# Second block's attention: two heads handled together, their score and value products issued in turns

## The chip, the cores and the metric

The kernel runs on one core of a Trainium2 chip. A core has a matrix engine (TensorE, called PE in the profile, with its weight loads listed apart as PEld), a vector engine (DVE), an activation engine (ACT), a small general engine (POOL) and a queue engine (SP) that starts most transfers from the chip's memory (HBM). Each engine has its own instruction queue and works through it in order; semaphores tie the queues together. The metric is the time in microseconds (us) that one execution takes on the device, and the median of several executions is compared.

## The reference

A sequence of 256 tokens of width 1024 in float32 runs through two layers of a first block and then one layer of a second block. The change touches the second block only. Cut to what matters there:

```python
# second_block, one layer: x is (256, 1024)
h = rmsnorm(x, g_mix_pre) * (1 + scale_m) + shift_m      # scale, shift, gate: from a condition vector
q, k, v, u = split(h @ w_in, 4)                           # each (256, 512)
# attention, 8 heads of width 64, strictly causal, "stick breaking":
z = q @ k.T / 8;  log1m = where(s < t, -softplus(z), 0)
after = reverse_cumsum(log1m) - log1m
w = where(s < t, exp(log_sigmoid(z) + after), 0)
attn = w @ v
# pooling: 4 groups of 128 channels of u, windows 2, 4, 8, 16
pooled[g] = trailing_mean(u[g], window[g]) - u[g];  pool[g] = (pooled[g] @ w_pool[g]) * pool_scale[g]
x = x + gate_m * rmsnorm(concat(attn, pool) @ w_out, g_mix_post)
h = rmsnorm(x, g_ffn_pre) * (1 + scale_f) + shift_f
x = x + gate_f * rmsnorm((silu(h @ w_gate) * (h @ w_up)) @ w_down, g_ffn_post)
```

## The kernel before

**Weights.** All large weights lie in HBM in one packed array, in the order of use (`ORDER`), in chunks of two halves of 128 x 1024. SP loads each half into one of 7 `raw` buffers (L258). ACT then makes a rounded copy H (L278) and DVE the rest L = raw - H (L280), each in one of 12 buffers, so that a product with a float32 weight is made of H and L parts in a faster matmul type. Activations are split the same way (`Pair`, L185 to L213). `get(key, cap)` (L284) hands out the next chunk, and on the way emits the loads up to 5 chunks ahead and the splits up to 3 chunks ahead, or up to the half numbered `cap` where one is given. `behind` (L262) makes the splits queue up after a named instruction of ACT (index 0) and of DVE (index 1), which is kept in `state["behind"]`.

**Order of the work.** The program's text is one long list of instructions. Small jobs that are to be woven into a long row of matmuls are generators: `spawn(gen, delay)` puts one on a list with a due time on a clock that `pe(ns)` moves on by an estimate of TensorE's time, and `tick()`, called between batches of matmuls, runs those that are due up to their next `yield`, whose value is the next delay. `drain()` runs all that is left. A scheduler then puts the instructions into the engines' queues by priority, which is their place in the text, and may let a later instruction that is ready go ahead of one that is not. `tc.high_priority(offset=PRIO)`, in the helper `hp`, moves instructions 30 places up.

**The second block's mixer** (`mixer2`, L981). For each half of the tokens, t = 0 and 1, `mmA4` makes q and then k (24 matmuls of 512 columns each, in batches of four H and two L). `turn` (L991) copies the result to memory on ACT (L993), transposes it on TensorE (L997) and copies it into `qT` or `kT` on DVE (L999). Then come v and u, for two halves of the tokens each (`pv`, `pu`), and into these rows of matmuls the eight heads are woven.

**A head** (`stick`, L938; `hp` is a pair of heads, `e` the head in it): two score matmuls into a PSUM tile `z`, with 64 rows of contraction, which lie on partitions 0 to 63 for e = 0 and 64 to 127 for e = 1; a mask addition on DVE (L949); Abs, Exp, Ln on ACT (L951 to L953); a combination on DVE (L955); three matmuls with a triangle of -1 (`tri`) that form the running sums in the same PSUM tile; Exp on ACT (L962) to `wT`. Each head is a generator of its own, spawned 3.5 clock units after the one before. When both of a pair are through, the value products are issued: all of e = 0, then all of e = 1, into the partitions 0 to 63 and 64 to 127 of one PSUM tile `po`. ACT and DVE put them, split, into the mixer's output `mp` (L211, L212).

**Pooling** (`pool`, L1024): for each of four groups in a row, a matmul pair into `pl`, a copy on ACT (L1031), a matmul with `wpool` into `ppl`, and a scaled split on ACT and DVE (L1037, L1038).

**After the mixer**: `w_out`, chunks of the pooled channels first (L1131), `drain()`, then the chunks of the attention's channels; norms; then the feed-forward part (`ffn`, L528). `gated` (L1107) loads a row of gains and a row of the modulation through ACT's DMA queue and multiplies them on DVE (128 x 1024). The last such row, `Pf`, is made before the feed-forward part starts (L1146) and is used only at its end. `ffn` has a parameter `early`, a function called at the seventh of the eleven chunks of the down product (L577); the first block's layers make their rows there.

Of the kernel before, what the change touches and what calls it, by code (L numbers as in the profile page):

```python
# [12 lines left out]
AF = mybir.ActivationFunctionType  # L13
# [5 lines left out]
P = 128  # L19
D = 1024  # L20
T = 256
# [4 lines left out]
HD = 64  # L26
# [22 lines left out]
UNIT = 10.0  # L49
SM_DELAY = 8.0  # L50
SOFT = 30
ST_DELAY = 7.0
ST_STEP = 3.5


# [107 lines left out]
def tile_model(ctx: ExitStack, tc: tile.TileContext, x_in, wpack, sink, convw, gains, c_in,  # L163
               b_cond, w_pool, pool_scale, ident_c, rope_c, amask_c, smask_c, tri_c, pmat_c, out):
    nc = tc.nc
# [7 lines left out]
    def s4(name, shape=(P, D), dt=F32):  # L173
        return ac.tile(list(shape), dt, tag="s4", name=name, bufs=NS4)

    def s2(name, shape=(P, 512), dt=F32):
        return ac.tile(list(shape), dt, tag="s2", name=name, bufs=NS2)

    def ps1(name, shape=(P, 512), dt=F32):
        return pp.tile(list(shape), dt, tag="B", name=name, bufs=8)  # L180
# [38 lines left out]
    def spawn(gen, delay=0.0):  # L219
        tasks.append([clock[0] + delay, gen])  # L220

    def pe(ns):
        clock[0] += ns / 1000.0
# [22 lines left out]
    def mm(o, a, b, start, stop, **kw):  # L246
        nc.tensor.matmul(o, a, b, start=start, stop=stop, **kw)  # L247


    state = dict(raw=0, spl=0, use=0, behind=None, a=None, v=None)  # L250
# [33 lines left out]
    def get(key, cap=None):  # L284

        i = state["use"]
        assert ORDER[i] == key, (ORDER[i], key)
        n = len(ORDER)
        while state["raw"] < 2 * min(i + LOOK_RAW, n):
            emit_raw()  # L290
        ahead = min(i + LOOK, n) * 2
        if cap is not None:
            ahead = max(min(cap, 2 * n), 2 * i + 2)
        while state["spl"] < ahead:
            emit_half()
        state["use"] += 1
        return HL.pop(i)
# [57 lines left out]
    def hp():  # L355
        return nullcontext() if state["use"] <= 4 else tc.high_priority(offset=PRIO)


    def sumsq(src, c, ssq, name):

        junk = s2(f"jk_{name}{c}")
        nc.scalar.activation(junk, src, AF.Square, scale=D ** -0.5, accum_out=ssq[:, c:c + 1])
        return nc.scalar.activation(ssq[:, c:c + 1], ssq[:, c:c + 1], AF.Identity,
                                    bias=eps if c == 0 else ssq[:, 0:1])
# [570 lines left out]
        return mp  # L935


    def stick(hp, qT, kT, v2, mp, psz, pend):  # L938
        ws = [None, None]

        def head(e):
            r = slice(e * HD, (e + 1) * HD)
            z = psz(hp, e)
            mm(z[:, 0:T], kT[r, hp, 0:P], qT[r, hp, :], True, False, skip_group_check=True)
            mm(z[:, T:T + P], kT[r, hp, P:T], qT[r, hp, P:T], False, False, skip_group_check=True)
            pe(650)
            zz = z[:, 0:384]
            z3 = zz.rearrange("p (b t) -> p b t", b=3)
            nc.vector.tensor_add(z3[:, 0:3:2, :], z3[:, 0:3:2, :], smask.unsqueeze(1).to_broadcast([P, 2, P]))  # L949
            e1 = s2(f"e1_{hp}{e}", (P, 384))  # L950
            nc.scalar.activation(e1, zz, AF.Abs)  # L951
            nc.scalar.activation(e1, e1, AF.Exp, scale=-1.0)
            nc.scalar.activation(e1, e1, AF.Ln, bias=1.0)  # L953
            spf = s2(f"sp{hp}{e}", (P, 384))
            nc.vector.scalar_tensor_tensor(spf, zz, 0.0, e1, ALU.max, ALU.add)  # L955
            yield ST_DELAY
            mm(z[:, 0:T], tri[:, 0, :], spf[:, 0:T], False, False, skip_group_check=True)
            mm(z[:, P:T], tri[:, 1, :], spf[:, T:T + P], False, False, skip_group_check=True)
            mm(z[:, T:T + P], tri[:, 0, :], spf[:, T:T + P], False, True, skip_group_check=True)
            pe(870)  # L960
            wT = s2(f"wT{hp}{e}", (P, 384))
            nc.scalar.activation(wT, zz, AF.Exp)  # L962
            ws[e] = wT
            yield 2.0
            if ws[0] is None or ws[1] is None or pend[hp]:
                yield None
                return
            pend[hp] = True
            po = ps1(f"po2{hp}")
            for ee in range(2):  # L970
                o = po[ee * HD:(ee + 1) * HD, :]
                vs = slice((2 * hp + ee) * HD, (2 * hp + ee + 1) * HD)
                mm(o[:, 0:T], v2[0][:, vs], ws[ee][:, 0:T], True, False, skip_group_check=True)
                mm(o[:, P:T], v2[1][:, vs], ws[ee][:, T:T + P], False, True, skip_group_check=True)
            pe(730)
            mp.put(hp, 1, po[:, 0:T].unsqueeze(1))
            yield None

        return [head(0), head(1)]

    def mixer2(xp, norms):  # L981
        mp = Pair("m2")
        qT = s4("qT2", (P, 4, T))
        kT = s4("kT2", (P, 4, T))
        v2t = s4("v2", (P, 2, 512))
        u2t = s4("u2", (P, 2, 512))
        v2 = [v2t[:, t, :] for t in range(2)]
        cap = 2 * state["use"] + 8
        ww = {n: [get((n, h), cap) for h in range(2)] for n in ("q2", "k2")}

        def turn(nm, t, ps, dstT, scl):  # L991
            tk = s2(f"tk2{nm}{t}")
            nc.scalar.activation(tk, ps, AF.Copy, scale=scl)  # L993
            yield 1.5
            pt = ps1(f"pt2{nm}{t}", (P, 4, P))
            for k in range(4):
                nc.tensor.transpose(pt[:, k, :], tk[:, k * P:(k + 1) * P], ident)  # L997
                pe(107)
            nc.vector.tensor_copy(dstT[:, :, t * P:(t + 1) * P], pt)  # L999
            yield None  # L1000

        for t in range(2):
            finish(norms[t].gen)
            for nm, dstT, scl in (("q2", qT, 0.125), ("k2", kT, 1.0)):
                ps = ps1(f"p2{nm}{t}")
                mmA4(ps, ww[nm], xp, t)
                spawn(turn(nm, t, ps, dstT, scl))
                tick()
        pend = [False] * 4

        def psz(hp, e):
            return ps1(f"z{hp}{e}")

        for hp in range(4):
            for e, gen in enumerate(stick(hp, qT, kT, v2, mp, psz, pend)):
                spawn(gen, 3.0 + ST_STEP * (2 * hp + e))
        for n, dst in (("v2", v2t), ("u2", u2t)):
            w = [get((n, h)) for h in range(2)]
            for t in range(2):
                ps = ps1(f"p{n}{t}")  # L1020
                mmA4(ps, w, xp, t)
                nc.scalar.copy(dst[:, t, :], ps)

        def pool(g):  # L1024
            pl = ps1(f"pl{g}")
            gs = slice(g * P, (g + 1) * P)
            mm(pl[:, 0:T], u2t[:, 0, gs], pmat[g // 2][:, g % 2, 0:T], True, False, skip_group_check=True)
            mm(pl[:, P:T], u2t[:, 1, gs], pmat[g // 2][:, g % 2, T:T + P], False, True, skip_group_check=True)
            pe(650)
            pm = s2(f"pm{g}", (P, T))  # L1030
            nc.scalar.copy(pm, pl[:, 0:T])  # L1031
            yield 1.5
            ps = ps1(f"ppl{g}")
            mm(ps[:, 0:T], wpool[:, g, :], pm, True, True)
            pe(432)
            h = mp.k(0, 4 + g)
            nc.scalar.activation(h, ps[:, 0:T], AF.Copy, scale=pscale[:, g:g + 1])  # L1037
            nc.vector.scalar_tensor_tensor(mp.k(1, 4 + g), ps[:, 0:T], pscale[:, g:g + 1],  # L1038
                                           h.bitcast(F32), ALU.mult, ALU.subtract)
            yield None  # L1040

        for g in range(4):
            for _ in pool(g):
                pass
        return mp


# [1 line left out]
    xp = Pair("x0")  # L1049
    norms = None  # L1050

    for l in range(DEPTH):
        mp = mixer1(l, xp, norms)
        gpm, gpf = row(4 * l + 1, f"gpm{l}"), row(4 * l + 2, f"gpf{l}")
        xp = Pair(f"xf{l}")
        norms = [Norm(t, gpf, None, xp, f"nf{l}{t}") for t in range(2)]
# [50 lines left out]
    def gated(gi, mi, name, one):  # L1107
        g = row(gi, "g" + name)
        m = s4("m" + name)
        nc.scalar.dma_start(m, modd[mi].partition_broadcast(P))  # L1110
        if one:
            nc.vector.scalar_tensor_tensor(g, m, 1.0, g, ALU.add, ALU.mult)
        else:
            nc.vector.tensor_mul(g, g, m)  # L1114
        return g

    mp = mixer2(xp, norms)
    xp = Pair("xf2")
# [4 lines left out]
    norms = [Norm(t, Gf, Sf, xp, f"nf2{t}") for t in range(2)]  # L1123
# [12 lines left out]
    cap = 2 * (state["use"] - 2) + NSPLIT  # L1136
    aw = [(get(("wo", 2, j), cap), mp.ks(0, 2 * j, 2), mp.ks(1, 2 * j, 2)) for j in (0, 1)]
    for t in range(2):
# [4 lines left out]
                mmD2(accs[t], *ch, t, c, len(left) == 2 and i == 0, ch is aw[1])  # L1143
            post.half(c)
        after3(t, post)
    Pf = gated(11, 5, "pf2", False)  # L1146

    def fin(t, post):
        def put(c):
            nc.sync.dma_start(out[t * P:(t + 1) * P, HC[c]], xt[t][:, HC[c]])  # L1150
        post.fin(put)

    ffn(2, xp, norms, lambda t, acc: Post(t, acc, Pf, f"pf2{t}"), fin)


def _consts():
# [56 lines left out]
```

## Time and profile before

| what | value |
|---|---|
| median of 3 executions | 1161.8 us (1160.68 to 1162.2) |
| the profiled execution, its own time | 1160.45 us |
| its span, first to last instruction | 1158.3 us |
| mean granted TensorE clock | 0.999 |
| PE busy / PEld busy | 1143.9 / 956.8 us |
| DVE busy / ACT busy | 801.3 / 687.5 us |
| transfers on SP's queue | 224.83 MB |

Times in the profile are counted from the span's start. A line of the timeline gives the start, the time until the last of the merged instructions ends, the engine, the source line, the operation, the tiles written and read (out<-in), the shape, how many were merged, and in brackets how long the engine sat idle before and what ended that. A matmul's shape begins with rows * columns of the array that it uses: `128*128` is the whole array, `64*128` half of its rows, `128*64` half of its columns. Nearly all matmuls stand under L247, a helper, so they are told apart by their tiles. A float32 matmul that is not split into H and L shows as two records.

### The profile page before, as it was taken

How to read it: one execution, taken by the hardware profiler on the slowest of the kernel's cores; microseconds unless marked ns; L12 is line 12 of the kernel's file. 1: busy time of each engine (PE TensorE's matmuls, PEld its weight loads, DVE VectorE, ACT ScalarE, POOL GpSimd, SP SyncE). 2: the span in 40 equal slices, each digit the busy share in tenths (PEclk: the TensorE clock that was granted, in tenths of full speed). 3: DMA queues.
4: the chain of work that ended last, by engine and by line, in shares of the span. 5: the costliest groups of instructions: out<-in, count | busy, mean ns of one | idle time of the engine just before them, and what ended most of it. 6: DMA issues, size and time to landing. Idle time of an engine off the chain costs nothing. (4 is left out here: it accounts for less than half of the span.)

```text
span 1158.3 us, 16004 instructions
## 1 busy us (share of the span) xinstructions
PE 1143.9 (99%) x5917; PEld 956.8 (83%) x5917; DVE 801.3 (69%) x1190; ACT 687.5 (59%) x1211; POOL 13.5 (1%) x28
## 2 busy tenths in 40 slices
PE   9999999999999999999999999999999999999997
PEld 5898888888888888888888888888887777888886
DVE  7888845858877647889855659966678437865642
ACT  6777865547545546688856456544556646645441
POOL 0000000000000000000000000000000000000000
PEclk9999999999999999999999999999999999999999
DMA  8934346737987854744575629977856343855600
GB/s 290 354 130 149 124 150 208 264 123 282 339 269 240 260 172 134 266 145 147 184 251 181 218 75 316 331 245 253 273 188 217 128 147 125 313 193 181 203 22 37
DMA packets 67039, 235.39 MB, mean 203 GB/s; under 512 B 8849, under 2 KB 9361, under 8 KB 66962
## 3 DMA queue, kind: packets, MB, share of 16 engines
q1 hardware_dynamic: 63216, 224.83, 56.9%
q10 hardware_dynamic: 3746, 9.56, 2.4%
q8 instruction: 46, 0.75, 0.3%
q14 instruction: 31, 0.25, 0.1%
HBM read 233.28 MB, written 1.07 MB: 202 GB/s over the span
## 5 line engine op out<-in xcount | busy, mean ns | idle before, releaser
L280 DVE TENSOR_TENSOR L<-raw,H 128x1024 fp32r<-128x1024 f32 x370 | 444.8, 1220 | 139.6 <-ACT H L278 132.0
L278 ACT CAST H<-raw 128x1024 fp32r<-128x1024 f32 x370 | 382.9, 1051 | 141.3 <-DMA raw<-in_wpack_dram 33.3
L247 PE MATMUL dn<-H,fHL 128*128 128x512 f32 x432 | 116.1, 390 | 0.0
L247 PE MATMUL pu<-xf,H 128*128 128x512 f32 x432 | 108.2, 392 | 0.0
L247 PE MATMUL pg<-xf,H 128*128 128x512 f32 x432 | 107.8, 391 | 0.0
L247 PEld LDWEIGHTS dn<-H,fHL 128*128 128x128 f32 x432 | 79.8, 188 | 15.6
L247 PEld LDWEIGHTS pg<-xf,H 128*128 128x128 f32 x432 | 79.2, 188 | 15.2
L247 PEld LDWEIGHTS pu<-xf,H 128*128 128x128 f32 x432 | 77.7, 189 | 13.9
L522 DVE SCALAR_TENSOR_TENSOR raw<-raw,silu_c 128x1024 f32<-128x1024 f32 x48 | 58.2, 1219 | 35.2 <-DMA raw<-in_wpack_dram 35.2
L247 PE MATMUL dn<-L,fHL 128*128 128x512 f32 x216 | 66.6, 389 | 0.0
L247 PEld LDWEIGHTS pg<-xf,L 128*128 128x128 f32 x432 | 58.9, 190 | 4.2
L247 PEld LDWEIGHTS pu<-xf,L 128*128 128x128 f32 x432 | 58.9, 190 | 4.2
L247 PE MATMUL pu<-xf,L 128*128 128x256 f32 x432 | 60.2, 282 | 0.0
L247 PE MATMUL pg<-xf,L 128*128 128x256 f32 x432 | 60.2, 282 | 0.0
L569 ACT CAST fHL<-f 128x512 fp32r<-128x512 f32 x27 | 16.7, 620 | 60.2 <-DVE f L567 60.2
L247 PE MATMUL wo<-H,m 128*128 128x512 f32 x192 | 52.3, 394 | 0.0
L563 ACT ACTIVATE s<-s 128x512 f32<-128x512 f32 x27 | 17.1, 631 | 54.6 <-DVE s L456 54.6
L247 PEld LDWEIGHTS dn<-L,fHL 128*128 128x128 f32 x216 | 40.5, 188 | 8.6
L247 PEld LDWEIGHTS wo<-H,m 128*128 128x128 f32 x192 | 35.5, 188 | 7.2 <-issue 0.2
L247 PE MATMUL pcp<-H,y 128*128 128x512 f32 x128 | 35.2, 395 | 0.0
L247 PE MATMUL pap<-H,o 128*128 128x512 f32 x128 | 35.1, 394 | 0.0
L664 ACT ACTIVATE P<-S,nm 128x256 f32<-128x256 f32 x64 | 29.6, 480 | 8.9 <-DVE nm L658 6.4
(290 smaller groups left out, 1950.3 us busy)
## 6 DMA issues: line engine op xcount, KB each, us to landing
raw<-in_wpack_dram SPq DMA_DIRECT2D x422, 512.0 KB, 5.4
gpm<-in_gains_dram ACTq DMA_DIRECT2D x3, 512.0 KB, 7.4
gpf<-in_gains_dram ACTq DMA_DIRECT2D x3, 512.0 KB, 8.9
gqf<-in_gains_dram ACTq DMA_DIRECT2D x2, 512.0 KB, 6.5
out_dram<-x SPq DMA_DIRECT2D x4, 256.0 KB, 2.0
pmat<-in_pmat_dram SPq DMA_DIRECT2D x2, 384.0 KB, 7.5
x<-in_x_dram SPq DMA_DIRECT2D x2, 256.0 KB, 2.9
x<-in_x_dram SPq DMA_DIRECT2D x1, 512.0 KB, 6.9
```

The lines of the kernel that those rows point to most:

```text
L247: nc.tensor.matmul(o, a, b, start=start, stop=stop, **kw)
L278: nc.scalar.copy(H, r)
L280: nc.vector.tensor_sub(L, r, H.bitcast(F32))
L522: nc.vector.scalar_tensor_tensor(w[u], w[u], 1.0, silu_c, ALU.mult, ALU.mult, accum_out=mcol[:, r, 2 * j + u:2 * j + u + 1])
L563: last = nc.scalar.activation(s, s, AF.Silu)
L569: nc.scalar.copy(fHL[:, 0], fv)
L664: nc.scalar.activation(Pt[:, hh, :], S[hh // 2][:, hh % 2, :], AF.Exp, bias=nm[:, hh:hh + 1], accum_out=den[:, hh:hh + 1])
```

## The change

The two heads of a pair become one generator. The score matmuls are issued e = 0, e = 1, e = 0, e = 1, and so are the value products. The three triangle matmuls of a head become two: one over 384 columns in place of one over 256 and one over 128. `spf` is written over `e1`. A pair is spawned every 7 units, as before on average, and the delay between scores and triangles is 8.0 in place of 7.0. In `turn`, the copies on ACT and DVE get the raised priority, and weight splits queue behind the copy on ACT. The split of v's weights is asked for in the first half of the tokens, right after k; u's weights are asked for after v's products and with a cap that ends at u's own halves, so `w_out`'s splits are emitted later than before. The first matmul pair of the next pooled group is issued before the second matmul of the current one. `Pf` is made through `early`.

```diff
-ST_DELAY = 7.0
+ST_DELAY = 8.0
...
+    ahead = hp
...
-    def stick(hp, qT, kT, v2, mp, psz, pend):
...
+    def stick(hp, qT, kT, v2, mp):
+
+        rs = [slice(e * HD, (e + 1) * HD) for e in range(2)]
+        z = [ps1(f"z{hp}{e}") for e in range(2)]
+        for e in range(2):
+            mm(z[e][:, 0:T], kT[rs[e], hp, 0:P], qT[rs[e], hp, :], True, False, skip_group_check=True)
+        for e in range(2):
+            mm(z[e][:, T:T + P], kT[rs[e], hp, P:T], qT[rs[e], hp, P:T], False, False, skip_group_check=True)
+        pe(900)
+        sps = []
+        for e in range(2):
...
-            spf = s2(f"sp{hp}{e}", (P, 384))
+            spf = e1
             nc.vector.scalar_tensor_tensor(spf, zz, 0.0, e1, ALU.max, ALU.add)
-            yield ST_DELAY
-            mm(z[:, 0:T], tri[:, 0, :], spf[:, 0:T], False, False, skip_group_check=True)
-            mm(z[:, P:T], tri[:, 1, :], spf[:, T:T + P], False, False, skip_group_check=True)
-            mm(z[:, T:T + P], tri[:, 0, :], spf[:, T:T + P], False, True, skip_group_check=True)
+            sps.append(spf)
+        yield ST_DELAY
+        ws = []
+        for e in range(2):
+            spf = sps[e]
+            mm(z[e][:, 0:384], tri[:, 0, :], spf, False, False, skip_group_check=True)
+            mm(z[e][:, P:T], tri[:, 1, :], spf[:, T:T + P], False, True, skip_group_check=True)
             pe(870)
             wT = s2(f"wT{hp}{e}", (P, 384))
-            nc.scalar.activation(wT, zz, AF.Exp)
-            ws[e] = wT
...
+            nc.scalar.activation(wT, z[e][:, 0:384], AF.Exp)
+            ws.append(wT)
+        yield 2.0
+        po = ps1(f"po2{hp}")
+        vs = [slice((2 * hp + e) * HD, (2 * hp + e + 1) * HD) for e in range(2)]
+        for e in range(2):
+            mm(po[rs[e], 0:T], v2[0][:, vs[e]], ws[e][:, 0:T], True, False, skip_group_check=True)
+        for e in range(2):
+            mm(po[rs[e], P:T], v2[1][:, vs[e]], ws[e][:, T:T + P], False, True, skip_group_check=True)
...
             tk = s2(f"tk2{nm}{t}")
-            nc.scalar.activation(tk, ps, AF.Copy, scale=scl)
+            with ahead():
+                state["behind"] = (nc.scalar.activation(tk, ps, AF.Copy, scale=scl), state["behind"][1])
...
-            nc.vector.tensor_copy(dstT[:, :, t * P:(t + 1) * P], pt)
+            with ahead():
+                nc.vector.tensor_copy(dstT[:, :, t * P:(t + 1) * P], pt)
...
+                if t == 0 and nm == "k2":
+                    wv = [get(("v2", h), cap + 4) for h in range(2)]
         for hp in range(4):
-            for e, gen in enumerate(stick(hp, qT, kT, v2, mp, psz, pend)):
-                spawn(gen, 3.0 + ST_STEP * (2 * hp + e))
+            spawn(stick(hp, qT, kT, v2, mp), 3.0 + 2 * ST_STEP * hp)
         for n, dst in (("v2", v2t), ("u2", u2t)):
-            w = [get((n, h)) for h in range(2)]
+            w = wv if n == "v2" else [get((n, h), cap + 8) for h in range(2)]
...
+        gens = [pool(g) for g in range(4)]
+        next(gens[0])
         for g in range(4):
-            for _ in pool(g):
-                pass
+            if g < 3:
+                next(gens[g + 1])
+            next(gens[g])
...
-    Pf = gated(11, 5, "pf2", False)
+    Pf = []
...
-    ffn(2, xp, norms, lambda t, acc: Post(t, acc, Pf, f"pf2{t}"), fin)
+    ffn(2, xp, norms, lambda t, acc: Post(t, acc, Pf[0], f"pf2{t}"), fin,
+        lambda: Pf.append(gated(11, 5, "pf2", False)))
```

More of the change, by code (lines that the diff above doesn't have):

```diff
@@ L935, in mixer1 @@
         return mp
-    def stick(hp, qT, kT, v2, mp, psz, pend):
[L939 to L947, printed above, removed]
+    def stick(hp, qT, kT, v2, mp):
[8 more added lines that the diff above has]
+        for e in range(2):
+            zz = z[e][:, 0:384]
             z3 = zz.rearrange("p (b t) -> p b t", b=3)
@@ L953, in head @@
             nc.scalar.activation(e1, e1, AF.Ln, bias=1.0)
-            spf = s2(f"sp{hp}{e}", (P, 384))
+            spf = e1
             nc.vector.scalar_tensor_tensor(spf, zz, 0.0, e1, ALU.max, ALU.add)
-            yield ST_DELAY
-            mm(z[:, 0:T], tri[:, 0, :], spf[:, 0:T], False, False, skip_group_check=True)
-            mm(z[:, P:T], tri[:, 1, :], spf[:, T:T + P], False, False, skip_group_check=True)
-            mm(z[:, T:T + P], tri[:, 0, :], spf[:, T:T + P], False, True, skip_group_check=True)
+            sps.append(spf)
[5 more added lines that the diff above has]
+            mm(z[e][:, P:T], tri[:, 1, :], spf[:, T:T + P], False, True, skip_group_check=True)
             pe(870)
             wT = s2(f"wT{hp}{e}", (P, 384))
-            nc.scalar.activation(wT, zz, AF.Exp)
-            ws[e] = wT
[L964 to L979, printed above, removed]
+            nc.scalar.activation(wT, z[e][:, 0:384], AF.Exp)
[7 more added lines that the diff above has]
+            mm(po[rs[e], P:T], v2[1][:, vs[e]], ws[e][:, T:T + P], False, True, skip_group_check=True)
+        pe(730)
+        mp.put(hp, 1, po[:, 0:T].unsqueeze(1))
+        yield None
     def mixer2(xp, norms):
@@ L1008, in mixer2 @@
                 tick()
-        pend = [False] * 4
-        def psz(hp, e):
-            return ps1(f"z{hp}{e}")
+                if t == 0 and nm == "k2":
+                    wv = [get(("v2", h), cap + 4) for h in range(2)]
         for hp in range(4):
-            for e, gen in enumerate(stick(hp, qT, kT, v2, mp, psz, pend)):
-                spawn(gen, 3.0 + ST_STEP * (2 * hp + e))
+            spawn(stick(hp, qT, kT, v2, mp), 3.0 + 2 * ST_STEP * hp)
         for n, dst in (("v2", v2t), ("u2", u2t)):
-            w = [get((n, h)) for h in range(2)]
+            w = wv if n == "v2" else [get((n, h), cap + 8) for h in range(2)]
             for t in range(2):
```

## The prediction

> **What bounds the kernel now.** The page comes first, for the busy times.
>
> ```profile
> span 1158.3 us, 16004 instructions
> PE 1143.9 (99%) x5917; PEld 956.8 (83%) x5917; DVE 801.3 (69%) x1190; ACT 687.5 (59%) x1211; POOL 13.5 (1%) x28
> ```
>
> TensorE is never idle for long, so a microsecond taken from its queue is a microsecond of the span, as long as no other engine's work becomes late for it. Whether that holds behind the mixer is read from the chain of waits in order of time: from the end back to 976 it is TensorE alone (and the last norm), and before that stands a piece of DVE:
>
> ```profile
> 973.62 1.23 DVE gpf L1114
> 974.84 1.15 DVE L L280
> 975.99 0.04 issue
> 976.03 3.44 PE puA L247 x14
> ```
>
> So time won in the mixer (866 to 942) is passed on to the end. What is left is to see how much of TensorE's time in the mixer is streaming and how much is entry, exit and waiting, and how full its helpers are. Busy time by stretches, the mixer from v's first product on and the feed-forward part:
>
> ```profile
> 890.30:942.00 51.70, 49.15 (x230) 36.67 (x229) 25.04 (x35) 30.63 (x55) 0.00 (x0) 1.00 0.46 163
> 990.60:1158.00 167.40, 160.84 (x845) 138.13 (x843) 92.18 (x114) 75.75 (x116) 1.10 (x2) 0.99 0.45 154
> ```
>
> (Columns: length; busy PE, PEld, DVE, ACT, POOL with counts; clock; DMA share; GB/s.) ACT is busy for 30.63 of 51.70 us there, DVE for 25.04: room, though not endless.
>
> **The change part by part.** TensorE's timeline gives each insertion's price: the time between the starts of the rows around it, less what these rows take undisturbed. First the undisturbed rows, with one insertion of value products behind them:
>
> ```profile
> 946.95 0.62 PE L247 MATMUL wo<-L,m 128*128 128x512 f32 x2
> 947.41 1.07 PE L247 MATMUL wo<-H,m 128*128 128x512 f32 x4
> 948.31 0.61 PE L247 MATMUL wo<-L,m 128*128 128x512 f32 x2
> 948.86 0.88 PE L247 MATMUL po<-wT,v 128*64 128x256 f32 x8
> 949.66 1.67 PE L247 MATMUL wo<-H,m 128*128 128x512 f32 x6
> 951.17 0.63 PE L247 MATMUL wo<-L,m 128*128 128x512 f32 x2
> ```
>
> Two L matmuls take 947.41 - 946.95 = 0.46 us and four H matmuls 0.90 undisturbed. The eight `po` records of the last pair were put into the queue in turns already, and both heads took 949.66 - 948.86 = 0.80 together; the way in cost 948.86 - 948.31 - 0.46 = 0.09, the way out 951.17 - 949.66 - 1.35 = 0.16 (six H matmuls would be 1.35): **1.05 us for a pair in turns**. The other pairs were not so:
>
> ```profile
> 911.75 1.04 PE L247 MATMUL z<-sp,tri 128*128 128x256 f32 x6
> 912.72 1.51 PE L247 MATMUL po<-wT,v 128*64 128x256 f32 x8
> 914.17 1.19 PE L247 MATMUL pu<-H,xm 128*128 128x512 f32 x4
> 915.20 0.63 PE L247 MATMUL pu<-L,xm 128*128 128x512 f32 x2
> ...
> 922.36 0.86 PE L247 MATMUL po<-wT,v 128*64 128x256 f32 x4
> 923.15 0.92 PE L247 MATMUL z<-qT,kT 64*128 64x256 f32 x4
> ...
> 924.42 0.86 PE L247 MATMUL po<-wT,v 128*64 128x256 f32 x4
> ...
> 932.14 0.86 PE L247 MATMUL po<-wT,v 128*64 128x256 f32 x4
> ...
> 934.00 0.86 PE L247 MATMUL po<-wT,v 128*64 128x256 f32 x4
> ```
>
> The first pair, one head after the other, took 914.17 - 912.72 = 1.45, with 0.09 in and 1.03 - 0.90 = 0.13 out: 1.67. Two pairs had their heads at different places, each 0.79 (923.15 - 922.36) + 0.09 + 0.13 = 1.01. **Value products**: before 1.67 + 4 x 1.01 + 1.05 = 6.8, after 4 x 1.05 = 4.2, a gain of 2.6.
>
> **Scores.** Each of the eight heads has an insertion of its own, on half of the rows of the array:
>
> ```profile
> 900.36 0.61 PE L247 MATMUL pv<-L,xm 128*128 128x512 f32 x2
> 900.90 0.92 PE L247 MATMUL z<-qT,kT 64*128 64x256 f32 x4
> 901.75 1.20 PE L247 MATMUL pv<-H,xm 128*128 128x512 f32 x4
> 902.79 0.62 PE L247 MATMUL pv<-L,xm 128*128 128x512 f32 x2
> ```
>
> That is 902.79 - 900.36 - 0.46 - 0.90 = 1.07 us, eight times 8.6. No row shows two heads on the two row halves in turns. Bounds from the nearest rows: if they overlap as the column halves do (0.80 for both against 0.79 for one), a pair costs 1.08, four cost 4.3, and the gain is 4.2. If the second head is streamed after the first, it adds what the second head of `po` added, 1.45 - 0.79 = 0.66; a pair costs 1.73, four cost 6.9, and the gain is 1.6, from half the entries alone. I take 4.2: the two halves are the same kind of split, and the heads write different PSUM tiles.
>
> In the Trainium skill, TensorE: Matmul & The Clock Gate, "The mechanism" of its part on packing, weight loads overlap running matmuls only where the row groups differ; the column halves above overlapped all the same, so the trace is the better judge here. The same page, "Measured speedup vs the span model", has four row tiles at 3.07 times, not 4. With the same share (1.53 of 2, an estimate from that page) a score pair would stream 2 x 0.85 / 1.53 = 1.11 in place of 0.85, and the gain would be 3.2 in place of 4.2.
>
> **Triangles.** Six records become four over the same 1024 columns (twice 256 + 128 + 128, twice 384 + 128). Six took 912.72 - 911.75 = 0.97 us, and `po`'s eight in sequence took 1.45 for 1536: in both 0.95 per 1000, so time goes with columns and the gain is 0. The other end: two records of six, 0.32 a head, 2.6 in all.
>
> **The wait for k's copy.** ACT's row, then TensorE's:
>
> ```profile
> 891.86 1.05 ACT L278 CAST H<-raw 128x1024 fp32r<-128x1024 f32 x1 [2.32 <-DMA raw<-in_wpack_dram]
> ...
> 894.10 0.59 ACT L993 ACTIVATE tk2k<-p2k 128x512 f32<-128x512 f32 x1
> ```
>
> ```profile
> 894.74 0.66 PE L997 MATMUL pt2k<-ident,tk2k 128*128 128x128 f32 x4 [1.61 <-ACT tk2k L993]
> ```
>
> The copy of k stood in ACT's queue behind splits that waited for a transfer, and the transposes stood at the head of TensorE's queue. With raised priority, and u's splits made to queue behind it, the copy comes first: gain 1.6, at worst 0. What is late next is u's splits: four pairs that wait until k's copy is through (about 890.3), needed when u starts, some 12 us later; ACT needs 4 x 1.05 for them. SP's queue keeps the order of its loads; while u's splits wait, its seven buffers stay full and the loads pause, which the DMA share of 0.46 in this stretch leaves room to make up. POOL's queue is not touched.
>
> **Pooled groups.** Two of the four second products waited:
>
> ```profile
> 939.59 0.70 PE L247 MATMUL ppl<-pm,wpool 128*128 128x256 f32 x2 [0.46 <-ACT pm L1031]
> ...
> 941.40 0.70 PE L247 MATMUL ppl<-pm,wpool 128*128 128x256 f32 x2 [0.46 <-ACT pm L1031]
> ```
>
> With the next group's first pair between, the wait is covered, except for the last group, which has only the group before it in front: 0.9 less about 0.2 is 0.7. Bounds 0 and 0.9.
>
> **The last gain row.** Its product is the 1.23 us of `gpf` in the chain above. It delays the split that TensorE waits for:
>
> ```profile
> 975.19 0.48 PE L247 MATMUL pgA<-H,xf 128*128 128x512 f32 x1
> 976.03 0.72 PE L247 MATMUL puA<-L,xf 128*128 128x512 f32 x2 [0.36 <-DVE L L280]
> ```
>
> A matmul that takes 0.23 (0.46 / 2) held the queue for 0.84: gain 0.6; the split would start 1.2 earlier, so nothing remains of this wait. Two DMA issues go from ACT's queue with it. At its new place DVE is busy for 92.18 of 167.40 us, and the splits are made three chunks ahead; that is the cover. Without it, the step can hold DVE as its model in the layer before did:
>
> ```profile
>   DMA scl_m<-modd: 8.1, 1
> ```
>
> 8.1 us of waiting for a row at L1078, ahead of which TensorE shows no wait. I take 0.
>
> **New waits.** The splits that move are the cost. ACT's casts (L278) by stretches:
>
> ```profile
> 878.00:890.30 12.30, 9.88 (x10) 1.00 0.63 194
> 890.30:942.00 51.70, 10.44 (x10) 1.00 0.46 163
> ```
>
> Of the ten before 890.3, v's four remain; u's four and w_out's first two come later. ACT then has 30.63 + 6 x 1.04 = 36.9 us in a stretch of 51.70 - 9.1 (the gains above without the last) = 42.6: 87%, DVE 25.04 + 6 x 1.22 = 32.4: 76%. A pair's chain runs through both. One head's, with two casts in between:
>
> ```profile
> 902.32 0.49 ACT L951 ACTIVATE e<-z 128x384 f32<-128x384 f32 x1 [0.69 <-DVE z L949]
> ...
> 905.32 0.52 ACT L953 ACTIVATE e<-e 128x384 f32<-128x384 f32 x1
> ```
>
> ```profile
> 906.59 0.55 DVE L955 SCALAR_TENSOR_TENSOR sp<-z,e 128x384 f32<-128x384 f32 x1
> ```
>
> From the end of the scores (901.75) to 907.14 are 5.4 us; the second head's three steps on ACT add 1.5, so 6.9, against a delay of 8.0 units. A slack of 1.1, about one cast. Bounds for the waits at the triangles: 0, and 4.0 (16 casts spread over four pairs are two more each, 2.1 - 1.1 = 1.0 a pair). I take 0.7, near the lower end, since w_out's splits come later in the text than the chains and yield to them.
>
> **Sum**: 4.2 + 2.6 + 1.6 + 0.7 + 0.6 - 0.7 = 9.0 us. The profiled execution took 1160.45, its span 1158.3: 1151.4 for such a one. It lies 1.35 below the median of the runs, so against the median: 1161.8 - 9.0 = **1152.8 us**.
>
> **The rivals.** *Row halves do not overlap.* For it: no row shows them together. Against it: the column halves do. The scores give 1.6 in place of 4.2: 1155.4.
>
> *ACT becomes the bound of the mixer.* For it: 87%, and one cast of slack per pair. Against it: u's splits have 12 us. The waits are 4.0 in place of 0.7: 1156.1.
>
> *The queue does not follow the text.* The last pair's value products went in turns though the text had them in sequence, so the scheduler's order counts, and it may cut a pair's insertion in two. Eight insertions cut would each cost a way in and out again, 0.09 + 0.13, and a first load of about 0.1: 8 x 0.3 = 2.6, so 1155.4.
>
> *Slower: the pair's chain is late at every pair.* Both heads' triangles now stand behind one chain that goes through ACT six times and through DVE ahead of and behind that. If on top of the four casts a pair also meets two of DVE's L (1.22 each), 1.0 + 2.4 = 3.4 us are exposed per pair, with TensorE's queue standing at the triangles: 4 x 3.4 = 13.8 against 9.7 gained: 1165.9. It decides from 9.7 / 4 = 2.4 us per pair on. Against it: v's and u's matmuls stand between scores and triangles by the due times, and splits of lower priority do not go first where a chain's step is ready.
>
> **How the numbers follow.** Forecast 0.55, row halves 0.18, ACT 0.14, cut insertions 0.05, slower 0.04; the last 0.04 for a gain of more than 11.5 (triangles cheaper by some of their 2.6). Range: below, no new waits and part of the triangles' gain, 1152.8 - 0.7 - 2.3 = 1149.8; above, past the rivals at 1155.4 and 1156.1, 1156.6. It leaves out the slower case and joint misses. About 0.2% (2.3 us) can be told from no change; faster 0.91 (all cases but the last and joint misses), same 0.05, slower 0.04.
>
> **What would show it.** Right: four score insertions `64*128` of eight records, with about 0.85 us from the start of one to the next row, and four `po` insertions of 0.80; no wait for `tk2k`; no DVE `gpf` ahead of `puA`; the mixer shorter by about 8 us, and the feed-forward part the same length. Row halves wrong: score insertions of 1.5. ACT: TensorE idle ahead of `z<-sp,tri` or `pu`, ended by L955, L953 or L280. Wrong altogether: a feed-forward part that starts earlier and then waits for splits.

## The result, and the profile after

The changed kernel takes 1149.42 us (median of 4 executions, 1148.9 to 1150.55) against 1161.24 us before (4 executions, 1160.56 to 1162.2). The ratio is 0.9906, with a 95% interval of 0.9895 to 0.9917, which is 9.6 to 12.2 us less; the two medians alone differ by 11.8. 1152.8 was forecast, 9.0 less than a median of 1161.8. The direction was right, and the gain was larger than the sum of its terms. As a time, 1149.42 lies 0.4 below the lower end of the stated range, 1149.8 to 1156.6. As a gain it lies inside: from 1161.8 that range is 5.2 to 12.0 us less. The profiled execution took 1148.9 us, its span 1146.9.

The head of the page of the changed kernel:

```profile
span 1146.9 us, 15965 instructions
...
PE 1135.7 (99%) x5901; PEld 951.2 (83%) x5901; DVE 799.9 (70%) x1190; ACT 686.9 (60%) x1211; POOL 13.4 (1%) x28
```

Sixteen matmul records fewer are the triangles. TensorE's own work fell by 8.2 us (1143.9 to 1135.7), and the span by 11.4, so some waiting went as well. Busy time by stretches (length; PE, PEld, DVE, ACT, POOL with counts; clock; DMA share; GB/s) of the changed kernel, from v's first product to the first of `w_out`, and the feed-forward part:

```profile
889.60:929.45 39.85, 39.78 (x205) 30.39 (x205) 27.67 (x37) 33.49 (x61) 0.00 (x0) 1.00 0.63 211
979.80:1147.00 167.20, 160.88 (x845) 138.17 (x843) 92.95 (x115) 75.45 (x116) 1.10 (x2) 0.99 0.47 159
```

The first stretch was 51.70 us long before and TensorE was busy for 49.15 of it; now it is 39.85 long and TensorE is idle for 0.07 of it. Not all of the difference is won: two pairs' value products now stand behind the first row of `w_out`, where one pair's stood before. The feed-forward part is as long as before. Where each stage begins is read from the first matmul record of its tile on TensorE's timeline, and the differences are what the experiments are compared by. All kernels in one table, in us, with the experiments that come below:

| kernel | v to u | u | u's end to w_out | w_out and norm | gate/up, first chunk | feed-forward | last matmul to end | q's first to end |
|---|---|---|---|---|---|---|---|---|
| before | 17.61 | 23.96 | 9.94 | 23.99 | 24.70 | 160.61 | 7.24 | 292.23 |
| changed | 13.51 | 19.78 | 6.54 | 25.85 | 24.37 | 160.61 | 6.62 | 281.55 |
| e1_sequence | 13.64 | 19.80 | 6.53 | 26.10 | 24.38 | 160.61 | 6.62 | 281.86 |
| e2_pairs_only | 15.21 | 19.78 | 8.81 | 25.02 | 24.89 | 160.61 | 7.23 | 285.73 |
| e3_rest_only | 15.39 | 24.34 | 7.75 | 25.49 | 24.33 | 160.62 | 6.62 | 288.72 |
| e4_pool_sequence | 13.52 | 19.78 | 8.81 | 25.02 | 24.30 | 160.62 | 6.62 | 282.86 |
| e5_same_due | 16.01 | 18.82 | 10.10 | 24.33 | 25.46 | 160.62 | 7.29 | 286.84 |
| e6_no_priority | 14.04 | 19.78 | 6.54 | 25.80 | 24.33 | 160.61 | 6.62 | 281.91 |
| e7_row_old_place | 13.52 | 19.78 | 6.53 | 25.83 | 25.31 | 160.61 | 7.25 | 283.02 |
| e8_apart | 15.53 | 21.20 | 8.92 | 27.05 | 24.36 | 160.62 | 6.63 | 288.49 |
| e9_row_only | 16.39 | 23.96 | 9.94 | 24.01 | 24.31 | 160.62 | 6.62 | 290.04 |
| e10_tighter_step | 15.17 | 19.35 | 6.49 | 23.96 | 24.35 | 160.62 | 6.61 | 280.74 |
| e11_changed_again | 13.51 | 19.78 | 6.54 | 25.83 | 24.31 | 160.62 | 6.61 | 281.48 |

The columns run from start to start: from the first `pv` to the first `pu`, on to the last `pu`, to the first `wo`, to the first `pgA`, to the first `pg`, to TensorE's last matmul, and from there to the end; the 24.2 to 24.3 us of q and k ahead of them are in the last column only. Each row is one execution; the changed kernel's two (changed and e11) differ by 0.07 in the last column. From q's first matmul on the change saves 292.23 - 281.55 = 10.68 us in these two executions; 0.7 more lies ahead of q, where nothing was changed, and moves by as much between executions of one kernel.

TensorE's timeline of the changed kernel, one pair's scores alone, and one pair's scores with the value products of another behind them:

```profile
900.25 0.61 PE L247 MATMUL pv<-L,xm 128*128 128x512 f32 x2
900.80 0.92 PE L247 MATMUL z<-qT,kT 64*128 64x256 f32 x8
901.65 1.20 PE L247 MATMUL pv<-H,xm 128*128 128x512 f32 x4
902.69 0.62 PE L247 MATMUL pv<-L,xm 128*128 128x512 f32 x2
...
904.53 1.90 PE L247 MATMUL z<-e,tri 128*128 128x384 f32 x8
...
908.58 0.61 PE L247 MATMUL pu<-L,xm 128*128 128x512 f32 x2
909.13 0.92 PE L247 MATMUL z<-qT,kT 64*128 64x256 f32 x8
909.98 0.87 PE L247 MATMUL po<-wT,v 128*64 128x256 f32 x8
910.78 1.19 PE L247 MATMUL pu<-H,xm 128*128 128x512 f32 x4
911.81 0.63 PE L247 MATMUL pu<-L,xm 128*128 128x512 f32 x2
...
934.37 0.62 PE L247 MATMUL wo<-L,m 128*128 128x512 f32 x2
934.92 0.65 PE L247 MATMUL po<-wT,v 128*64 128x256 f32 x2
935.50 1.20 PE L247 MATMUL wo<-H,m 128*128 128x512 f32 x4
936.53 0.62 PE L247 MATMUL wo<-L,m 128*128 128x512 f32 x2
...
939.58 0.86 PE L247 MATMUL po<-wT,v 128*64 128x256 f32 x6
```

Eight score records take 901.65 - 900.80 = 0.85 us, the time that four took before, and the whole insertion 902.69 - 900.25 - 0.46 - 0.90 = 1.08. The two row halves overlap to within 0.01 us. Where the value products stand right behind the scores (twice), the two share one way in and out: 911.81 - 908.58 - 0.46 - 0.90 = 1.87 for both, where 1.08 + 1.05 = 2.13 was forecast. Against that, one pair's value products are cut in two, two records at 934.92 and six at 939.58.

The chain of waits of the changed kernel where it reaches the feed-forward part, in order of time:

```profile
960.54 1.41 DVE xg_nf L395 x2
961.96 1.15 DVE L L280
963.10 0.04 issue
963.15 3.52 PE puA L247 x14
```

`gpf` is gone from it; DVE's split L follows the norm directly.

### The profile page after: what moved, and what is told of

The parts are those of the page before. It is cut to its first block, busy times and chain, and to the rows that moved or that the text cites. A ratio compares the mean times of both kernels' runs of the same rounds, so it can differ in the third digit from the quotient of the medians.

```text
span 1146.9 us, 15965 instructions
## 1 busy us (share of the span) xinstructions
PE 1135.7 (99%) x5901; PEld 951.2 (83%) x5901; DVE 799.9 (70%) x1190; ACT 686.9 (60%) x1211; POOL 13.4 (1%) x28
## 3 DMA queue, kind: packets, MB, share of 16 engines
HBM read 233.28 MB, written 1.07 MB: 204 GB/s over the span
```

## The experiments

**e1_sequence: the changed kernel without the turns.** Within each pair all of e = 0 is issued, then all of e = 1.

```diff
             mm(z[e][:, 0:T], kT[rs[e], hp, 0:P], qT[rs[e], hp, :], ...)
-        for e in range(2):
             mm(z[e][:, T:T + P], kT[rs[e], hp, P:T], qT[rs[e], hp, P:T], ...)
...
             mm(po[rs[e], 0:T], v2[0][:, vs[e]], ws[e][:, 0:T], ...)
-        for e in range(2):
             mm(po[rs[e], P:T], v2[1][:, vs[e]], ws[e][:, T:T + P], ...)
```

> The changed kernel with the score products and the value products of a pair one head after the other, all else as in it; the heads stay in pairs. If the overlap of the array's halves carries the gain: a score insertion of eight records takes 0.85 + 0.66 = 1.51 us to the next row in place of 0.85, a value insertion 1.45 in place of 0.80, so 4 x 0.66 + 4 x 0.65 = 5.2 us are lost and the time is about 1154.6 (beside 1149.4 for the changed kernel and 1161.2 for the one before). Rival, that fewer insertions and the moved splits carry it: less than 1 us is lost, at most 1150.4.

Measured: 1149.79 us, ratio to before 0.9908 (0.9893 to 0.9923), like the changed kernel; in the table 0.3 us are lost, not 5.2. Its score insertion on TensorE's timeline, and then the view of the tile `z` for the window 901.0 to 901.6 alone (count, durations in ns, first and last start, shapes):

```profile
900.57 0.61 PE L247 MATMUL pv<-L,xm 128*128 128x512 f32 x2
901.12 0.93 PE L247 MATMUL z<-qT,kT 64*128 64x256 f32 x8
901.98 1.20 PE L247 MATMUL pv<-H,xm 128*128 128x512 f32 x4
903.02 0.62 PE L247 MATMUL pv<-L,xm 128*128 128x512 f32 x2
```

```profile
L247 PE MATMUL z<-qT,kT x4: 376/428/480, 901.1 to 901.5; 64*128 64x256 f32 x4
```

0.86 us for both heads, 1.09 with way in and out. TensorE's queue of this kernel, as the program is built, holds in this order head 0 over 256 columns, head 0 over 128, head 1 over 256, head 1 over 128, each as two records. Yet in the first half of the insertion only records over 256 columns start, four of them: both heads'. Head 1's first matmul thus starts ahead of head 0's second, which stands before it in the queue. The order in turns buys nothing; TensorE runs the two halves of the array beside each other when the matmuls of both stand next to each other in its queue.

The Trainium skill, TensorE: Matmul & The Clock Gate, "The mechanism", says that matmuls start and end strictly in queue order. For the starts of matmuls on two halves of the array these rows show otherwise.

**e8_apart: the changed kernel with the heads pulled apart.** A yield between the two heads' scores, and between their value products, lets other batches of matmuls in.

```diff
-        for e in range(2):
             mm(z[e][:, T:T + P], kT[rs[e], hp, P:T], qT[rs[e], hp, P:T], ...)
-        pe(900)
+            pe(450)
+            if e == 0:
+                yield 0.5
...
-        for e in range(2):
             mm(po[rs[e], P:T], v2[1][:, vs[e]], ws[e][:, T:T + P], ...)
-        pe(730)
+            pe(365)
+            if e == 0:
+                yield 0.5
```

> The changed kernel with the two heads of a pair pulled apart: a yield of 0.5 units between the first and the second head's scores, and between their value products, so that a batch of v's or u's matmuls stands between them. If standing next to each other is the cause: eight score insertions of 1.07 us in place of four of 1.08 and eight value insertions of 1.01 in place of four, 4.2 + 3.9 = 8.1 us longer than the changed kernel, about 1157.5 beside 1149.4. Rival, that TensorE reaches over a batch of full-array matmuls, or that the pairs gain by something else: less than 2 us longer.

Measured: 1156.54 us, ratio 0.9961 (0.9947 to 0.9975); in the table 288.49 - 281.55 = 6.9 us are lost, with 8.1 expected. TensorE's timeline:

```profile
895.50 0.92 PE L247 MATMUL z<-qT,kT 64*128 64x256 f32 x4
896.34 1.19 PE L247 MATMUL pv<-H,xm 128*128 128x512 f32 x4
...
897.94 0.92 PE L247 MATMUL z<-qT,kT 64*128 64x256 f32 x4
898.78 1.19 PE L247 MATMUL pv<-H,xm 128*128 128x512 f32 x4
```

One head alone takes 0.84 us, two together took 0.85. Standing next to each other is what the paired heads gain. Of the 1.2 us short of the expectation, 0.4 is that two value products stand right before scores here and share the way in and out; the rest is not placed.

**e5_same_due: the kernel before with one line changed.** Each head keeps its own generator; only the two of a pair fall due together.

```diff
-                spawn(gen, 3.0 + ST_STEP * (2 * hp + e))
+                spawn(gen, 3.0 + 2 * ST_STEP * hp)
```

> The kernel before with one line changed: both heads of a pair are spawned with the same due time, 3.0 + 7.0 per pair, so that their insertions stand next to each other in TensorE's queue, one head after the other; no turns, no other part of the change. The run with the pair in sequence lost nothing, so the new theory is that two halves of the array overlap whenever their matmuls stand next to each other with operands ready, whatever the order. Then the scores give 4.2 and the value products 2.6: 6.8 us less than before. Rival, that the pair needs its own generator and delays: less than 3 us gained.

Measured: 1155.03 us, ratio 0.995 (0.9935 to 0.9965), 5.4 us less in the table, with 6.8 expected. All four score insertions hold eight records, and so do the four of value products. It stays 1.1 behind e2, which has the same pairs in one generator, although its wait for k's copy happened to be 0.9 shorter (below under e6). On TensorE it shows its triangles and two late groups of value products:

```profile
904.70 1.92 PE L247 MATMUL z<-sp,tri 128*128 128x256 f32 x12
...
909.08 1.09 PE L247 MATMUL po<-wT,v 128*64 128x256 f32 x8
...
926.95 1.25 PE L247 MATMUL po<-wT,v 128*64 128x256 f32 x8 [0.49 <-ACT wT L962]
```

These two groups take 910.11 - 909.08 = 1.03 and 928.12 - 926.95 = 1.17 to the next row, where 0.80 is the price of two ready heads. Head 1's first record starts 0.23 and 0.38 after head 0's (909.31 and 927.33), just after ACT has finished its `wT` (909.26 and 927.27). So a group is longer by as much as its second head is late. With the 0.49 in brackets that is 1.1 us.

Its triangles are the old form, twelve records for a pair in 1.92 us. The new form has eight in 1.90 (the changed kernel at 904.53, above). So fewer, wider triangle matmuls are worth 0.02 us a pair.

**e2_pairs_only and e3_rest_only: the change in two.** e2 is the kernel before with the new `stick`, its `spawn` and `ST_DELAY = 8.0`; e3 is the rest without them (`turn`, the weights of v and u, the pooled groups, `Pf`).

> The kernel before with the heads in pairs and in turns alone (delay 8.0); priorities, order of splits, pooled groups and the last gain row as before. By the prediction's sum 4.2 + 2.6 = 6.8 us less than before, about 1154.4, with the waits for k's copy (1.6), in pooling (two of 0.46) and behind the gain row (0.36) still in the trace. Rival, that the other parts carry most: 4 us or less, 1157 or more.

> The kernel before with all the other parts (priorities, order of splits, pooled groups, last gain row) and its old heads. By the prediction's sum 1.6 + 0.7 + 0.6 = 2.9 us less than before, about 1158.3. If the parts add up, this and the run with the pairs alone give together what the whole change gave, 11.8; if they fall short by 1.5 or more, something in the whole change gains that neither part has alone, such as value products that share their entry with scores.

Measured: e2 1152.88 us, ratio 0.9936 (0.992 to 0.9953); e3 1157.04 us, ratio 0.9969 (0.9959 to 0.9979). In the table 6.50 and 3.51 us less; together 10.0 of the 10.68. By the ratios (0.64% and 0.31% against 0.94%) the parts add up, so the missing 0.7 is not clear of noise. What would explain it is seen in the traces: in e2 all four pooled groups wait, as in the next experiment, and two did in the kernel before.

**e4_pool_sequence: the changed kernel with the pooled groups one after the other.**

```diff
-        gens = [pool(g) for g in range(4)]
-        next(gens[0])
         for g in range(4):
-            if g < 3:
-                next(gens[g + 1])
-            next(gens[g])
+            for _ in pool(g):
+                pass
```

> The changed kernel with the pooled groups one after the other as before. By the prediction 0.7 us longer. By the trace of the changed kernel, in which the waits of both groups (start to start 0.63 each) are gone, 1.3 longer in the pooling, but the last pair's value products, which the changed kernel issues in two pieces (two records, later six), stand together in this one's queue, which saves about 0.8 in w_out's part: 0.5 longer from the first score to the end of w_out. Rival, that the cut does not come with the pooling: 1.3 longer.

Measured: 1150.39 us (one execution). The four second products, first of this kernel, then of the changed one:

```profile
926.22 0.70 PE L247 MATMUL ppl<-pm,wpool 128*128 128x256 f32 x2 [0.24 <-ACT pm L1030]
...
928.03 0.70 PE L247 MATMUL ppl<-pm,wpool 128*128 128x256 f32 x2 [0.46 <-ACT pm L1030]
...
929.84 0.70 PE L247 MATMUL ppl<-pm,wpool 128*128 128x256 f32 x2 [0.46 <-ACT pm L1030]
...
931.66 0.70 PE L247 MATMUL ppl<-pm,wpool 128*128 128x256 f32 x2 [0.46 <-ACT pm L1030]
```

```profile
926.32 0.59 PE L247 MATMUL ppl<-pm,wpool 128*128 128x256 f32 x2
...
927.41 0.60 PE L247 MATMUL ppl<-pm,wpool 128*128 128x256 f32 x2
...
928.50 0.60 PE L247 MATMUL ppl<-pm,wpool 128*128 128x256 f32 x2
...
929.15 0.67 PE L247 MATMUL ppl<-pm,wpool 128*128 128x256 f32 x2
```

With the paired heads fewer pieces of triangles are left to stand between the groups, so in sequence all four second products wait (1.62 us in brackets), not two as before. Putting the next group's first pair between removes all four: 8.81 - 6.54 = 2.27 us. Of that 25.85 - 25.02 = 0.83 is lost again behind it, where e4 has both remaining insertions of value products whole and the changed kernel has one cut. Net 1.4, and 1.3 in the last column; 0.5 was expected, from two waits.

**e6_no_priority: the changed kernel with `turn` as it was.**

```diff
             tk = s2(f"tk2{nm}{t}")
-            with ahead():
-                state["behind"] = (nc.scalar.activation(tk, ps, AF.Copy, scale=scl), state["behind"][1])
+            nc.scalar.activation(tk, ps, AF.Copy, scale=scl)
...
-            with ahead():
-                nc.vector.tensor_copy(dstT[:, :, t * P:(t + 1) * P], pt)
+            nc.vector.tensor_copy(dstT[:, :, t * P:(t + 1) * P], pt)
```

> The changed kernel without the raised priority of the copies in turn and without the splits queued behind them; the split order stays. If the priority removed the wait for k's copy: six splits stand ahead of that copy again, TensorE waits 1.6 us for it, and v's products end 1.6 us later. Rival, that the earlier request of v's splits and the later one of u's removed it: no wait, no difference.

Measured: 1149.48 us (one execution), 0.36 us more in the table. The wait for k's copy in e6, and then in e2, e5 and e9, whose program is that of the kernel before up to this point, each from TensorE's timeline:

```profile
892.97 0.65 PE L998 MATMUL pt2k<-ident,tk2k 128*128 128x128 f32 x4 [0.31 <-ACT tk2k L994]
```

```profile
895.06 0.66 PE L998 MATMUL pt2k<-ident,tk2k 128*128 128x128 f32 x4 [1.49 <-ACT tk2k L994]
```

```profile
893.85 0.66 PE L997 MATMUL pt2k<-ident,tk2k 128*128 128x128 f32 x4 [0.61 <-ACT tk2k L993]
```

```profile
893.98 0.66 PE L997 MATMUL pt2k<-ident,tk2k 128*128 128x128 f32 x4 [0.41 <-ACT tk2k L993]
```

With the 1.61 of the kernel before, the same wait was 0.41, 0.61, 1.49 and 1.61 us in four executions. What varies is when the raw halves land for which the casts ahead of the copy wait: on ACT those waits add up to 1.87, 2.08, 2.94 and 3.08 us in the same four. ACT's timeline of e6 ahead of the copy:

```profile
891.37 1.05 ACT L278 CAST H<-raw 128x1024 fp32r<-128x1024 f32 x1 [1.26 <-DMA raw<-in_wpack_dram]
892.33 0.59 ACT L994 ACTIVATE tk2k<-p2k 128x512 f32<-128x512 f32 x1
```

In e6, as in the kernel before, six casts stand between q's copy and k's, and transfers hold some of them. So asking for the splits at another place does not bring the copy forward, and the rival falls; the raised priority, with the splits queued behind the copy, does. The 1.6 us that were expected did not come back in this execution, 0.31 did. In the changed kernel the copy comes ahead of these casts, and no transfer holds it (ACT's timeline):

```profile
889.84 0.60 ACT L995 ACTIVATE tk2k<-p2k 128x512 f32<-128x512 f32 x1 [5.33 <-PE p2k L247]
890.34 7.67 ACT L278 CAST H<-raw 128x1024 fp32r<-128x1024 f32 x8
```

**e7_row_old_place and e9_row_only: the last gain row.** e7 is the changed kernel with `Pf` made ahead of the feed-forward part; e9 is the kernel before with only `Pf` moved. The edit of e9 (e7 is its reverse):

```diff
-    Pf = gated(11, 5, "pf2", False)
+    Pf = []
...
-    ffn(2, xp, norms, lambda t, acc: Post(t, acc, Pf, f"pf2{t}"), fin)
+    ffn(2, xp, norms, lambda t, acc: Post(t, acc, Pf[0], f"pf2{t}"), fin,
+        lambda: Pf.append(gated(11, 5, "pf2", False)))
```

> The changed kernel with the last gain row made before the feed-forward part, as before. By the prediction 0.6 us longer between the first pgA and the first pg matmul. By the two traces, in which this stretch is 24.70 us before and 24.36 after, 0.3 longer, because the wait for the first L of uA grew when the second went. Rival: nothing.

> The kernel before with one edit: the last gain row is made through the parameter of the feed-forward part, at its seventh chunk. If the row's product was a cost only by delaying the split that TensorE waits for (the prediction's term of 0.6), the stretch from the first pgA to the first pg is shorter by the two waits of 0.31 and 0.36 that TensorE shows there, 0.5 to 0.9 us, and the time from TensorE's last record to the end stays at 7.24: total 1160.5 to 1160.7 against 1161.2. If the shorter tail belongs to the row's place as well, that time falls to 6.62 too, and the whole gain is 1.1 to 1.5: about 1159.9.

Measured: e7 1150.4 us (one execution); e9 1158.68 us, ratio 0.9983 (0.9973 to 0.9992). e9's gain holds about 1.2 us by which k's copy happened to come earlier (0.41 against 1.61); what is left in the table is 24.70 - 24.31 = 0.39 ahead of the feed-forward part and 7.24 - 6.62 = 0.62 behind its last matmul. In e7, DVE first waits for the row's transfer and only then multiplies, and TensorE waits longer:

```profile
963.72 1.23 DVE L1116 TENSOR_TENSOR gpf<-gpf,mpf 128x1024 f32<-128x1024 f32 x1 [0.60 <-DMA mpf<-modd]
...
966.14 0.73 PE L247 MATMUL puA<-L,xf 128*128 128x512 f32 x2 [0.96 <-DVE L L280]
```

so there the old place costs 25.31 - 24.37 = 0.94 (0.3 expected) and the same 0.63 at the end. One wait stays whatever the place of the row, at the first `puA`, here of the kernel before and then of the changed one:

```profile
973.67 0.73 PE L247 MATMUL puA<-L,xf 128*128 128x512 f32 x2 [0.31 <-DVE L L280]
```

```profile
963.15 0.74 PE L247 MATMUL puA<-L,xf 128*128 128x512 f32 x2 [0.65 <-DVE L L280]
```

**e10_tighter_step and e11_changed_again: without the cut.** e10 is the changed kernel with two constants, e11 the changed kernel unedited beside it.

```diff
-ST_DELAY = 8.0
-ST_STEP = 3.5
+ST_DELAY = 7.0
+ST_STEP = 3.25
```

> The changed kernel with ST_STEP 3.25 and ST_DELAY 7.0 (before the edit 3.5 and 8.0). By the order of its instructions no pair's value products are cut in two, and the last pair's stand in u's rows or late in w_out as one piece of eight. The cut cost 0.83 us in the changed kernel, so if nothing becomes late, a gain of 0.3 to 0.8: 1148.6 to 1149.1 beside the changed kernel's 1149.4. If a pair's chain is late under the shorter delay, TensorE shows a wait at z<-e,tri, up to 1 us for each pair, and the time is 1149.5 to 1152.

> The changed kernel itself, unedited, on the same chip as the two others, for comparison with e10: 1149.4, within 0.6.

Measured: e10 1148.82 us (4 executions, 1148.34 to 1149.02), ratio to before 0.9896 (0.9878 to 0.9913); e11 1149.23 us (1148.76 to 1149.94), 0.99 (0.9883 to 0.9918). All of e10's value products are whole; from the first `wo` on it is 25.85 - 23.96 = 1.89 us shorter, partly because one insertion less lies there, and 0.8 in all in the table. The medians differ by 0.4 in the expected direction, which is less than can be told from no change.

## Why the prediction was right, and where it was not

**What bounds the kernel**: right. Every microsecond taken from the mixer arrived at the end; the feed-forward part is 160.61 or 160.62 in all kernels.

**Scores**: right, 1.08 a pair as forecast, and the row halves overlap like the column halves. The rival that they don't would have shown 1.5 us of streaming; 0.85 is there. The old price, eight times 1.07, was read from one insertion; another of the eight stands in two pieces in that trace (896.71 and 897.76) and cost 1.46. The Trainium skill, TensorE: Matmul & The Clock Gate, "Measured speedup vs the span model", has 3.07 for four row tiles, from which the prediction estimated 1.11 us of streaming for two halves; the 0.85 here does not bear that out.

**Value products**: the mechanism named was wrong, the size nearly right. The step said that the last pair's records "were put into the queue in turns already", and took 1.05 as the price "for a pair in turns". That queue had head 0 first and head 1 after it, as in the text, and e1 shows that the order makes no difference. The first pair took 1.45 for another reason: head 1's `wT` was late. ACT's timeline of the kernel before:

```profile
912.83 0.49 ACT L962 ACTIVATE wT<-z 128x384 f32<-128x384 f32 x1 [0.39 <-PE z L247]
```

It ends at 913.32, 0.60 after `po`'s first matmul at 912.72; head 1's matmuls start at 913.37, 0.65 after head 0's, and the group is 1.45 - 0.80 = 0.65 longer. So the price of 1.05 belongs to two heads that stand together *and are both ready*; the two groups of e5 above, with 0.23 and 0.38, lie between. That the sum came out nearly right is luck: the change provides both, and not for the reason given. The rival that the queue does not follow the text had its support from the same misreading. The insertions of scores and value products after: 1.08 twice, 1.87 and 1.89 for the two shared ones, 1.03 for a whole `po`, 0.80 and 1.01 for the cut one, 8.8 us in all against 8.5 forecast. A cut, which a rival priced at 0.3, came for one pair and cost 0.80 + 1.01 - 1.03 = 0.78, and the shared ways in and out, which no term had, gave 0.5 back. Gain 15.4 (the forecast's count of the old insertions) - 8.8 = 6.6, with 6.8 forecast. The 6.5 of e2 is made up otherwise: no cut, and two more waits in pooling.

**k's copy**: the wait went as said, 1.6 in this pair of executions. Mis-sized as a term against a median: the 1.61 was one execution's, and the four seen have a mean of 1.0.

**Pooled groups**: 0.7 forecast, about 1.3. The term took the 0.46 in brackets for each of the two waits. From start to start they cost more: the row ahead of a waiting second product takes 939.59 - 938.31 = 1.28 in the kernel before and 927.41 - 926.75 = 0.66 in the changed one, so 0.62 each, and the last group waits no more either. Nor did the term see that pairing the heads adds two waits by taking the triangles from between the groups; against those the edit is worth a net 1.3 as well (e4).

**The gain row**: 0.6 forecast, 0.39 (e9) or 0.94 (e7) ahead of the feed-forward part, and 0.62 at the end, which nobody looked for. "Nothing remains of this wait" holds for the `puA` that the step named; the `puA` before it, which the step left out, waits 0.65 where it waited 0.31.

**New waits**: -0.7 forecast, none seen; that and the rivals on ACT and on late chains fall together. ACT had the load that was foreseen, 33.49 of 39.85 us (84%, forecast 87%), without TensorE waiting once between v and `w_out`. What covers it, v's and u's matmuls by the due times or w_out's splits yielding, was not tried.

**Triangles**: 0 forecast, 0.02 a pair. The two rows that were compared for it each held something else: the 0.97 the step over to half of the array (alone, the six take 907.85 - 907.06 = 0.79 in the kernel before), the 1.45 the late head.

**Sum**: the mis-sized terms are +0.7 for the waits that did not come, +0.6 for the pooled groups, +0.4 to 1.0 for the row, -0.2 for the insertions: 1.5 to 2.1, against 10.68 - 9.0 = 1.7 in the table.

## What to carry to other kernels

Matmuls that use only half of the array's rows or columns should stand right next to those of the other half, with both sides' operands ready (a second half that is late adds its delay); their order among themselves is free, and one changed due time gave about half of this change's gain. A wait that a transfer sets should be read from several executions before it becomes a term. When several edits are summed, ask what each takes away from the cover of the others: the pooled groups' waits doubled once the heads were paired.

## What was not expected of the hardware

TensorE started a matmul on one half of the array ahead of an earlier one in its queue on the other half (e1: four records over 256 columns ahead of those over 128; 0.86 us against 0.85 in turns).

The tail behind the last matmul is about 0.6 us shorter in every kernel that makes the gain row late (6.61 to 6.63) than in those that make it early (7.23 to 7.29), though the product ends far ahead of it: 176 us before the last matmul in the kernel before, 29 in the changed one. SP's waits in the last microseconds, of the kernel before and of the changed one (total, times, longest):

```profile
SPq L1209 <- DMA out_dram<-x: 2.1, 1, 2.1
```

```profile
SPq L1212 <- DMA out_dram<-x: 1.6, 1, 1.6
```

The last output store is waited for 0.5 us less. e9 shows that the row's place alone does it; why is open.
